# Retention queries projected with channels on partitions, rotary tables from plain transposes, decays moved into the norm's constant and the values

## The chip, the cores and the metric

The kernel runs on one core of a Trainium2 chip. A core has five engines with instruction streams of their own: PE (TensorE, matrix products and transposes), DVE (VectorE), ACT (ScalarE), POOL (GpSimd) and SP (SyncE, which here only issues DMAs). On-chip memory has 128 partitions; PE writes into PSUM, of which the kernel uses eight banks of 128 x 512 floats. The metric is the device time of one execution in microseconds, lower is better; a kernel's time is the median of its runs.

## The reference

Two layers of a decoder trunk on one sequence of 1024 tokens with 1024 channels. In each layer a normed and modulated h (1024 x 1024) goes through one projection whose columns feed three head groups: A, sliding-window attention with rotary; B, retention; C, gated linear attention. The gated outputs are joined, projected by `w_out`, normed, scaled by a gate and added to x. The part that the change touches is retention, with 4 heads of 64 channels and chunks of 128 tokens:

```python
rq = apply_rotary(rq.reshape(B, S, RET_HEADS, RET_DK), positions, ret_freq)
rk = apply_rotary(rk.reshape(B, S, RET_HEADS, RET_DK), positions, ret_freq)
r = retention(rq, rk, rv.reshape(B, S, RET_HEADS, RET_DV))
r_out = rms_norm(r).reshape(B, S, RET_W) * jax.nn.silu(rg)
# retention, per chunk and head, gamma = 1 - 2**(-5 - head), k scaled by 64**-0.5:
dmask = jnp.where(diff >= 0, jnp.exp(log_g[:, None, None] * jnp.maximum(diff, 0.0)), 0.0)
sc = jnp.einsum('bhid,bhjd->bhij', qi, ki) * dmask
intra = jnp.einsum('bhij,bhjv->bhiv', sc, vi)
inter = jnp.einsum('bhid,bhdv->bhiv', qi * q_decay, state)
new_state = chunk_decay * state + jnp.einsum('bhjd,bhjv->bhdv', ki * k_decay, vi)
```

`apply_rotary` turns each head's two halves of 32 channels by the token's angle: (x1 cos - x2 sin, x2 cos + x1 sin). The decay between token j and token i of a chunk is gamma**(i - j), so it can be split into a factor of i and a factor of j.

## The kernel before, in words

**Tiles.** The 1024 tokens are 8 tiles of 128 (`t`), or 4 pairs (`p`), or 2 halves (`hf`). h is kept transposed, channels on partitions, as a high and a low float32r part (`hT[(l, p)]`, 256 tokens per pair); the weights are split the same way, in blocks of 256 columns. Every projection is three passes (high x high, low x high, high x low; `PASSES`, L608) over 8 blocks of 128 channels, 24 products for one result.

Two forms of projection exist. `project` (L619) keeps h in the array and streams the weights: the result has 128 tokens on partitions and 256 channels along the row. `project_T` (L626) keeps 128 columns of the weights and streams 512 tokens: the result has channels on partitions.

**The order of a layer** (`layer`, L1466): output gates of C and B (`do_gates`), the retention pairs, C's projections and cores, keys and values of A, A's queries (`attn_rot`, L859), A's gates, then the output projection. In the last layer that product is done by a Strassen-like scheme in `last_output`.

**Who sets the order.** PE's instructions run in the order in which the program writes them down. This order comes from a small planner in the program: `clk` adds up a cost of each PE instruction (`mult`, L164; `transp`, L179), and generators (`job`) give back by `yield` how long after their last step their next PE step is due; the delays stand in the table `L` (L1677). `pump()` (L210) is called every 7 products inside a projection and runs the jobs that are due. `flag` and `await_flag` tie steps to one another: a `yield (0.0, name)` waits for a flag. On the other engines the compiler orders instructions by its own estimate, within the order of priority in which the program writes them. SP's queue takes its issues in order, each when its buffers are ready.

**Buffers.** `t2` (128 x 512, 10 of them), `t1` (128 x 256, 8), `st` (staging for weights, 5), `mm` (3 PSUM banks for projections), `aux` (5 banks for the rest), `mix_tile` (two large tiles), and `kT0`, `kT1` (one each of 128 x 1024, in turn for x, gaT, A's keys and the sums of the last layer).

**Tables.** `tables` (L411) works out sine and cosine of all angles into `sincos` (token on partition; for each tile sine then cosine, 32 rotary columns of A, then 32 of B), with 16 DVE operations of 512 columns on four `t2` tiles and two on ACT. `tables_T` (L444) makes A's tables with channels on partitions: for each pair a DVE copy repeats the 32 columns for 4 heads (L449), four transposes (L455), a copy on ACT with the factor 0.125 (L457), and a store into `tabS` in DRAM (L458). `attn_rot` loads them back in halves, two DMAs of 256 KB a time (L864). A's queries then are turned as whole banks: bank times cosine (L870), bank times sine (L871), a difference (L873), a sum (L874), a copy on ACT (L877); four DMAs of 32 partitions swap the halves into place (`qst`, L880).

**Retention** (L1502 to L1520). For each pair, the blocks rq, rk and rv are projected in this order, two tiles each, token on partition. `ret_rot` (L1154) turns a tile of q or k by `rotary` (L817: five DVE operations, L823 to L828) and multiplies it by its decay (L1157): gamma**(i+1) for q (`qdec`), 0.125 gamma**-(i+1) for k (`kdec`). A tile of v is copied by ACT. After each tile of v the job `ret_core` (L1160) starts:

```python
        for j in range(2):
            transp(pt[:, j * P:(j + 1) * P], q[:, j * P:(j + 1) * P], ident)
            transp(pt[:, (2 + j) * P:(3 + j) * P], k[:, j * P:(j + 1) * P], ident)
        tt_ = t2()
        ...
        copy("rT", tt_, pt)
```

ACT copies the four transposes into `tt_`, the scores k'q are made with 64 rows each (L1175), DVE masks them (L1179), PE adds scores x v and q x state (L1187, L1189), makes the state's increment (L1194), and DVE adds it and decays the state. `head_norm_gate` (L970) squares, reduces, makes the reciprocal root (`rstd_of`, L632, with a constant epsilon) and multiplies by the gate.

After the last tile of each block the next weights are asked for: `load` (L508) puts four pieces on a queue; each piece is a DMA of 256 KB into an `st` tile, a conversion to the high part (L149, ACT or DVE) and a subtraction to the low part (L533, DVE or POOL).

## Time and profile before

| | |
|---|---|
| median of 3 runs (lowest, highest) | 996.02 us (995.09, 997.33) |
| the profiled execution, its own time | 996.31 us |
| its span, first to last instruction | 994.6 us |
| granted TensorE clock, mean | 0.991 |
| transposes of `t` tiles on PE | 292 |
| DMAs issued: loads from `tabS`, swaps of q's halves | 16, 32 |
| SP queue, share of 16 DMA engines | 44.5% |

The prediction quotes rows of the profile. In a row of a group stand line, engine, operation, output<-input, shapes and count, then busy microseconds and the mean nanoseconds of one, then the engine's idle time before them with what ended it. A row of the timeline or of the chain starts with start and length in microseconds from the start of the span; x4 means four instructions merged. A row of the waits gives total microseconds, number of times and the longest. A row of stretches gives the stretch, its length, the busy time and instruction count of PE, PEld (the loading of the stationary operand), DVE, ACT and POOL, then the clock, the DMA share and GB/s. Matmuls overlap, and their ends are modelled: their pace is read from starts, not from durations.

### The profile page before, as it was taken

To read this page: it belongs to the slowest core of one execution; us is meant where nothing else is said; L and a number is where in the kernel's file an instruction comes from. 1 tells how busy PE (TensorE), PEld (TensorE's weight loads), DVE (VectorE), ACT (ScalarE), POOL (GpSimd) and SP (SyncE) were. 2 spreads that over 40 slices of the span, in tenths; PEclk is the share of its full clock that TensorE was granted. 3 is DMA by queue.
4 is the path that set the end of the run, shared out by engine and by line. 5 is a ranking of instruction groups with operands and counts; after the bars stand their busy time and mean duration, and the time that the engine had idled before them with its cause. 6 is when DMAs were issued, how large, how long until landed. Compare 5 with 4: busy or idle time off the path is not lost.

```text
span 994.6 us, 19641 instructions
## 1 busy us (share of the span) xinstructions
PE 965.7 (97%) x7133; PEld 824.3 (83%) x7133; DVE 683.2 (69%) x1679; ACT 409.3 (41%) x1152; POOL 246.3 (25%) x310
## 2 busy tenths in 40 slices
PE   5899999999999999999999999999999999999996
PEld 1599999888998777778889999988999877777785
DVE  3779857677766777664677286775766577567876
ACT  2477312233332656632555332133333257574222
POOL 2322001233310234420124101113322034545000
PEclk8899999999999999999999999999999999999999
DMA  9843513523135355587555241352122434378883
GB/s 321 290 138 97 159 44 115 177 86 121 61 100 166 91 157 168 170 274 239 189 170 171 69 150 38 118 157 83 53 93 86 127 91 133 112 235 266 267 262 139
DMA packets 112305, 148.77 MB, mean 150 GB/s; under 512 B 12065, under 2 KB 63821, under 8 KB 112209
## 3 DMA queue, kind: packets, MB, share of 16 engines
q1 hardware_dynamic: 106512, 137.96, 44.5%
q10 hardware_dynamic: 5696, 9.56, 2.6%
q8 instruction: 56, 0.92, 0.4%
q14 instruction: 41, 0.33, 0.1%
HBM read 109.20 MB, written 36.18 MB: 146 GB/s over the span
## 4 chain that ended last, share of the span: by engine, by line
PE 80%; DVE 7%; DMA 7%; issue 2%; POOL 1%; ACT 1%; SPq 0%; ACTq 0%; POOLq 0%; DVEq 0%
PE mm L165 61%; PE aux L165 14%; PE aux L180 5%; DMA st<-in_w_in_dram 2%; POOL sm L635 1%; DMA t<-aoS 1%; DMA st<-in_w_last_dram 1%; DMA xk<-in_x_dram 1%; DVE arena L533 1%; DMA a<-mixS 1%; DVE t L1248 0%; DVE t L328 0%; DMA t<-in_x_dram 0%; DMA t<-xs 0%; DMA mixS<-t 0%
## 5 line engine op out<-in xcount | busy, mean ns | idle before, releaser
L165 PE MATMUL mm<-arena 128*128 128x256 f32 (+2 forms) x1824 | 299.9, 318 | 1.8 <-ACT arena L704 1.8
L165 PE MATMUL mm<-arena,arena 128*128 128x256 f32 (+2 forms) x1824 | 298.2, 316 | 0.0
L165 PEld LDWEIGHTS mm<-arena 128*128 128x128 f32 x1824 | 255.5, 191 | 26.0 <-issue 3.3
L165 PEld LDWEIGHTS mm<-arena,arena 128*128 128x128 f32 x1824 | 252.2, 188 | 24.3 <-issue 3.7
L635 POOL TENSOR_TENSOR sm<-sm,mhalf 128x1 f32<-128x1 f32 (+1 forms) x64 | 55.8, 872 | 335.9 <-DVE sm L634 317.8
L165 PE MATMUL mm<-arena,mx 128*128 128x512 f32 (+1 forms) x564 | 130.6, 387 | 0.5 <-ACT kept L1341 0.5
L165 PEld LDWEIGHTS mm<-arena,mx 128*128 128x128 f32 x564 | 101.4, 188 | 24.7 <-issue 1.9
L149 ACT ACTIVATE t<-aux 128x256 f32<-128x256 f32 (+2 forms) x124 | 55.8, 468 | 73.8 <-PE aux L180 62.2
L149 ACT ACTIVATE arena<-st 128x512 fp32r<-128x512 f32 x94 | 56.2, 627 | 53.2 <-DMA st<-in_w_in_dram 19.4
L929 POOL TENSOR_TENSOR smx<-smx,sm 128x512 f32<-128x512 f32 x32 | 36.1, 1129 | 125.7 <-DVE sm L928 118.0
L533 POOL TENSOR_TENSOR arena<-st,arena 128x512 fp32r<-128x512 f32 x31 | 42.7, 1378 | 79.7 <-ACT arena L149 72.9
L533 DVE TENSOR_TENSOR arena<-st,arena 128x512 fp32r<-128x512 f32 x77 | 58.0, 775 | 5.2 <-ACT arena L149 3.3
L925 ACT ACTIVATE smx<-smx,sm 128x129 f32<-128x129 f32 x128 | 49.9, 393 | 25.9 <-DVE sm L922 25.7
L364 DVE SCALAR_TENSOR_TENSOR acc<-st,c_act,acc 128x512 f32<-128x512 f32 x60 | 46.7, 778 | 16.9 <-DMA st<-in_w_mod_dram 16.5
L180 PE MATMUL aux<-c_ident,t 128*128 128x128 f32 (+1 forms) x292 | 48.2, 282 | 5.4 <-DVE t L666 5.0
L180 PEld LDWEIGHTS aux<-c_ident,t 128*128 128x128 f32 (+1 forms) x292 | 35.0, 144 | 12.4 <-DVE t L666 6.9
L698 ACT ACTIVATE t<-aux,mod,mod 128x128 f32<-128x128 f32 x68 | 25.9, 459 | 43.0 <-DVE t L1248 18.1
L165 PEld LDWEIGHTS aux<-t,mx 32*128 32x128 f32 (+1 forms) x896 | 39.5, 187 | 3.9 <-issue 2.1
L973 ACT ACTIVATE t<-aux 128x256 f32<-128x256 f32 x32 | 12.3, 383 | 73.6 <-PE aux L165 65.0
L165 PE MATMUL aux<-t,mx 32*128 32x32 f32 (+1 forms) x896 | 40.7, 272 | 0.0
L920 DVE COPY_PREDICATED smx<-c_curmask,aux 128x256 f32<-128x256 int32 x64 | 25.4, 446 | 19.5 <-ACT smx L149 17.2
L1248 DVE SCALAR_TENSOR_TENSOR t<-t,sm,t 128x512 f32<-128x512 f32 x32 | 24.0, 780 | 18.2 <-DMA t<-in_x_dram 10.8
(224 smaller groups left out, 1387.7 us busy)
## 6 DMA issues: line engine op xcount, KB each, us to landing
st<-in_w_in_dram SPq DMA_DIRECT2D x96, 256.0 KB, 3.8
st<-in_w_mod_dram SPq DMA_DIRECT2D x64, 256.0 KB, 3.1
mx<-mixS SPq DMA_DIRECT2D x20, 512.0 KB, 4.9
mixS<-t SPq DMA_DIRECT2D x72, 128.0 KB, 3.7
st<-in_w_last_dram SPq DMA_DIRECT2D x36, 256.0 KB, 3.8
wm<-in_w_mod_dram SPq DMA_DIRECT2D x12, 512.0 KB, 7.0
t<-in_x_dram SPq DMA_DIRECT2D x24, 256.0 KB, 4.9
t<-tabS SPq DMA_DIRECT2D x16, 256.0 KB, 4.6
```

The source lines that it names most:

```text
L149: A.activation(dst, src, AF.Copy)
L165: T.matmul(dst, lhsT, rhs, start=start, stop=stop)
L180: T.transpose(dst, src, idn)
L364: V.scalar_tensor_tensor(acc, wt, c_act[:, k:k + 1], acc, ALU.mult, ALU.add)
L533: e.tensor_tensor(lo, st, f(hi), ALU.subtract)
L635: G.tensor_tensor(r, r, mhalf[:, :w], ALU.pow)
L698: A.activation(hf[:, ks], at[kt], AF.Identity, scale=gain, bias=shift)
L920: V.copy_predicated(sv, curmask.unsqueeze(1).to_broadcast((P, 2, P)), pv[:, :, n // P - 1, :])
L925: A.activation(sm[:, h, :], sm[:, h, :], AF.Exp, bias=mx[:, h:h + 1], accum_out=sums[:, h:h + 1])
L929: eng("pn").tensor_tensor(sm[:, :, 0:128], sm[:, :, 0:128], rs.unsqueeze(2).to_broadcast((P, 4, P)), ALU.mult)
L973: A.activation(sq, po, AF.Square)
L1248: V.scalar_tensor_tensor(xt[j], yg[j], r, xt[j], ALU.mult, ALU.add)
```

## The change

Six parts:

1. **q of retention** is projected by a new form, `project_P`: 128 columns of the weights in the array, 256 tokens of the pair streaming, two results in the two halves of one bank. The columns of rq are permuted on the host, so that the first result holds the first halves of all heads and the second the second halves. `ret_q` turns the bank with tables in four DVE operations, ACT copies it to a tile `rqT` (in the buffers kT0 for pairs 0 and 1, kT1 for pairs 2 and 3), and four DMAs (`qst`) swap the halves so that each head's 64 channels lie together. A flag falls due 6.5 planner units later (`rq1`).
2. **`ret_core`** transposes k alone, ACT copies 256 columns, and the scores and the product with the state read q from `rqT`, behind a wait for that flag.
3. **Decays.** q and k are no longer multiplied by a decay. v is, on DVE, by gamma**-(i+1) (`vdec`), in place of ACT's copy. The factor of i goes into the norm's epsilon, 4 EPS gamma**(-2(i+1)) (`reps`), since the head norm divides a common factor out; 0.125 comes with the tables.
4. **Tables** are transposed as `sincos` holds them: 8 transposes of 128 x 128 in two groups, two ACT copies, two stores into `tabS`, now 128 rows (sine for A, sine for B, cosine for A, cosine for B, 32 each) by 1024 tokens. The DVE copies (L449) are gone. A load repeats 32 rows for four groups of 32 partitions, with four DMAs (`tab_load`): eight of 64 KB in `attn_rot`, eight of 32 KB in `ret_q`.
5. **The work tiles of `tables`** come out of one `mix_tile` instead of four `t2`, and its first operation is put behind the last modulation on DVE (`mark[3]`).
6. **Delays** in `L`: `tb1` 24.5 to 20.0, `tt1` 8.0 to 3.0, `tt2` 1.75 to 2.0, `rq1` 6.5 new.

The core of the diff:

```diff
-    c["qdec"] = (gam[None, :] ** (i[:, None] + 1.0)).astype(f)
-    c["kdec"] = (0.125 * gam[None, :] ** (-(i[:, None] + 1.0))).astype(f)
+    c["reps"] = (4.0 * EPS * gam[None, :] ** (-2.0 * (i[:, None] + 1.0))).astype(f)
+    c["vdec"] = (gam[None, :] ** (-(i[:, None] + 1.0))).astype(f)
...
-        ang = t2()
-        V.tensor_tensor(ang.rearrange("p (t k) -> p t k", t=NT), posf.unsqueeze(2).to_broadcast((P, NT, 64)),
-                        freq.unsqueeze(1).to_broadcast((P, NT, 64)), ALU.mult)
+        tmp = mix_tile(F32).rearrange("p a k q -> p (a k q)").rearrange("p (i n) -> p i n", i=4)
+        ang, nn, n2, red = (tmp[:, i] for i in range(4))
+        with tc.issue_after(mark[3].ins):
+            V.tensor_tensor(ang.rearrange("p (t k) -> p t k", t=NT), posf.unsqueeze(2).to_broadcast((P, NT, 64)),
+                            freq.unsqueeze(1).to_broadcast((P, NT, 64)), ALU.mult)
...
+        for i in range(2):
+            yield L["tt1"] if i == 0 else L["tt2"]
             pt = aux()
-            for i in range(4):
-                transp(pt[:, i * P:(i + 1) * P], rep_[:, i * P:(i + 1) * P], ident)
+            for t in range(4):
+                transp(pt[:, t * P:(t + 1) * P], sincos[:, 4 * i + t].rearrange("p s k -> p (s k)"), ident)
             tb = t2()
             A.activation(tb, pt, AF.Copy, scale=0.125)
-            nc.sync.dma_start(tabS[p], tb.rearrange("p (s n) -> p s n", s=2))
+            nc.sync.dma_start(tabS[:, 512 * i:512 * i + 512], tb)
...
+    def project_P(pm, l, p, w, c):
+        h = hT[(l, p)]
+        accum(pm, lambda a, k: w[:, a, k, c:c + P], lambda b, k: h[:, b, k, 0:256])
...
+    def tab_load(d, r, c, n):
+        for h in range(4):
+            nc.sync.dma_start(d[32 * h:32 * h + 32], tabS[r:r + 32, c:c + n])
...
         for s, d in ((0, sn), (1, cs)):
-            nc.sync.dma_start(d.rearrange("p (s n) -> p s n", s=2),
-                              tabS[2 * hf:2 * hf + 2, :, s, :].rearrange("s p n -> p s n"))
+            tab_load(d, 64 * s, 512 * hf, 512)
...
+    def ret_q(l, p, w):
+        tab = t2()
+        for i in range(2):
+            tab_load(tab[:, 256 * i:256 * i + 256], 64 * i + 32, 256 * p, 256)
+        pm = mm()
+        for c in range(2):
+            project_P(pm[:, 256 * c:256 * c + 256], l, p, w, c * P)
...
+        u, x = t2(), t2()
+        V.tensor_tensor(two(u), two(pm), cs, ALU.mult)
+        V.tensor_tensor(two(x), two(pm), sn, ALU.mult)
+        V.tensor_tensor(u[:, 0:256], u[:, 0:256], x[:, 256:512], ALU.subtract)
+        V.tensor_tensor(u[:, 256:512], u[:, 256:512], x[:, 0:256], ALU.add)
+        if p % 2 == 0:
+            rqT[0] = gp.tile([P, NT * P], F32, tag=f"kT{p // 2}", name=nm("rq"), bufs=1)
+        q = rqT[0][:, 512 * (p % 2):512 * (p % 2) + 512]
+        A.activation(q, u, AF.Copy)
+        q, u = two(q), two(u)
+        for j in range(2):
+            for r in range(2):
+                dst, src = 64 * r + 32 * (1 - j), 64 * r + 32 * j
+                dma("qst", q[dst:dst + 32, j], u[src:src + 32, 1 - j])
+        flag(("rq", l, p), L["rq1"])
+        return q
...
         for j in range(2):
-            transp(pt[:, j * P:(j + 1) * P], q[:, j * P:(j + 1) * P], ident)
-            transp(pt[:, (2 + j) * P:(3 + j) * P], k[:, j * P:(j + 1) * P], ident)
-        tt_ = t2()
...
-        copy("rT", tt_, pt)
+            transp(pt[:, j * P:(j + 1) * P], k[:, j * P:(j + 1) * P], ident)
+        kTt = t1()
+        copy("rT", kTt, pt[:, 0:256])
+        yield (0.0, ("rq", l, t // 2))
...
-        yield from head_norm_gate(l, t, po[:, 0:256], sg, 4.0 / 64.0, 4.0 * EPS, 4)
+        yield from head_norm_gate(l, t, po[:, 0:256], sg, 4.0 / 64.0, reps, 4)
...
+            q = ret_q(l, p, used(l, "rq"))
+            pump()
+            if last:
+                load(l, "gqk")
+            ks = {}
+            for name in ("rk", "rv"):
...
                     if name == "rv":
                         v = t1()
-                        copy("rv", v, src)
-                        job(ret_core(l, t, rr[("rq", tt)], rr[("rk", tt)], v))
+                        V.tensor_tensor(h4(v), h4(src), vdec.unsqueeze(2).to_broadcast((P, 4, 64)), ALU.mult)
+                        job(ret_core(l, t, q, ks[tt], v))
                     else:
-                        rr[(name, tt)] = ret_rot(t, src, qdec if name == "rq" else kdec)
+                        ks[tt] = ret_k(t, src)
...
+    icols[RQ:RQ + 256] = RQ + np.arange(256).reshape(2, 2, 2, 32).transpose(2, 1, 0, 3).reshape(-1)
```

More of the change, by code (lines that the diff above doesn't have):

```diff
@@ L262, in trunk @@
     srS = dr.tile([NT, P, 256], F32, name="srS")
-    tabS = dr.tile([NP_, P, 2, 256], F32, name="tabS")
+    tabS = dr.tile([P, S], F32, name="tabS")
     modc = {}
@@ L429, in tables @@
         yield
-        red = t2()
         for i, cv in enumerate(cw_consts(1.0)):
@@ L767, in trunk @@
     hmask = cload("hmask")
-    qdec = cload("qdec")
-    kdec = cload("kdec")
+    reps = cload("reps")
+    vdec = cload("vdec")
     cdt = cload("cdt")
@@ L1151, in gla_out, with two, ret_k @@
         yield from head_norm_gate(l, t, po, gate, 1.0 / 64.0, EPS, 6)
-    def ret_rot(t, src, dec_):
+    def ret_q(l, p, w):
[5 more added lines that the diff above has]
+            project_P(pm[:, 256 * c:256 * c + 256], l, p, w, c * P)
+        def two(x):
+            return x.rearrange("p (c n) -> p c n", c=2)
+        sn, cs = (tab[:, 256 * i:256 * i + 256].unsqueeze(1).to_broadcast((P, 2, 256)) for i in range(2))
+        u, x = t2(), t2()
[14 more added lines that the diff above has]
+        return q
+    rqT = [None]
+    def ret_k(t, src):
         r = t1()
         rotary(r, src, 4, t, 1)
-        eng("rdec").tensor_tensor(h4(r), h4(r), dec_.unsqueeze(2).to_broadcast((P, 4, 64)), ALU.mult)
         return r
@@ L1503, in layer @@
             last = p == NP_ - 1
-            rr = {}
-            for name in ("rq", "rk", "rv"):
+            q = ret_q(l, p, used(l, "rq"))
[4 more added lines that the diff above has]
+            for name in ("rk", "rv"):
                 w = used(l, name)
@@ L1513, in layer @@
                         v = t1()
[L1514 to L1515 removed]
+                        V.tensor_tensor(h4(v), h4(src), vdec.unsqueeze(2).to_broadcast((P, 4, 64)), ALU.mult)
+                        job(ret_core(l, t, q, ks[tt], v))
                     else:
[L1517 removed]
+                        ks[tt] = ret_k(t, src)
                     pump()
                 if last:
[L1520 removed]
+                    load(l, {"rk": "gv", "rv": "kv"}[name])
         G.memset(stC, 0.0)
```

24 lines of the change are left out of this document (8 added, 16 removed).

## The prediction

> **What bounds the kernel now.** I read the page first: engines, then the chain that ended last.
>
> ```profile
> PE 965.7 (97%) x7133; PEld 824.3 (83%) x7133; DVE 683.2 (69%) x1679; ACT 409.3 (41%) x1152; POOL 246.3 (25%) x310
> ...
> PE 80%; DVE 7%; DMA 7%; issue 2%; POOL 1%; ACT 1%; SPq 0%; ACTq 0%; POOLq 0%; DVEq 0%
> ```
>
> PE is busy 97% of the span and makes 80% of the chain. So what PE is given to do counts almost in full, and what the other engines do counts only where PE waits for them. Next the weight-load row of PE in the timeline, around the ends of the two retention stages, which shows where PE waits there.
>
> ```profile
> 192.83 0.52 PEld L165 LDWEIGHTS aux<-t 64*128 64x128 f32 x8 [1.73 <-ACT t L149]
> ...
> 663.09 0.52 PEld L165 LDWEIGHTS aux<-t 64*128 64x128 f32 x8 [0.75 <-ACT t L149]
> ...
> 669.66 0.52 PEld L165 LDWEIGHTS aux<-t 64*128 64x128 f32 x8 [1.41 <-ACT t L149]
> ```
>
> These are the score products of `ret_core` (64 rows), which wait for ACT's copy of the transposes (the `rT` copy): 1.73 + 0.75 + 1.41 = 3.9 us in all. The chain of waits tells why ACT was late:
>
> ```profile
> 186.23 1.00 DVE arena L533 x2
> 187.24 4.07 DMA st<-in_w_in_dram
> ...
> 191.39 0.06 ACT arena L149
> ...
> 191.93 0.86 ACT t L149 x2
> ```
>
> DVE splits a weight block late, only then is the staging tile free, the next weight block takes 4.07 us to arrive, ACT stands at its conversion, and the `rT` copy is queued behind that. The fourth pair of each retention stage, taken as one stretch each, shows DVE nearly full:
>
> ```profile
> 166.30:187.20 20.90, 20.90 (x183) 20.51 (x183) 18.50 (x54) 6.02 (x13) 5.55 (x4) 1.00 0.42 133
> ...
> 641.00:662.00 21.00, 21.00 (x184) 20.76 (x182) 16.78 (x50) 5.98 (x13) 3.84 (x4) 1.00 0.38 119
> ```
>
> The third column after the length is DVE: 18.50 of 20.90 us and 16.78 of 21.00. PE has no pause in either stretch; its clock is full.
>
> **The change part by part.**
>
> *PE.* The transposes of q go: 2 of 4 in each `ret_core`, 16 of them (8 tiles, 2 layers), so 32. The tables need 8 transposes for 16. That is 40 fewer.
>
> ```profile
> L180 PE MATMUL aux<-c_ident,t 128*128 128x128 f32 (+1 forms) x292 | 48.2, 282 | 5.4 <-DVE t L666 5.0 <-DVE mx L1121 0.2
> ```
>
> ```profile
> 97.26 0.44 PE aux L180 x4
> ...
> 120.17 0.44 PE aux L180 x4
> ```
>
> The group gives 282 ns for one, but 292 x 282 would be 82 us and the group is busy 48.2: they overlap. The chain shows the pace: four of the tables take 0.44 us (97.26), and four in `ret_core` too (120.17), 0.11 us each. 40 x 0.11 = **-4.4 us**. The Trainium skill, page "TensorE: Matmul & The Clock Gate", section "Part 4: PE-mode transpose", gives about 275 ns for one in a kernel's context; as a duration the 282 ns agree with it, and by it as a cost the sum would be 40 x 0.275 = -11 us, an estimate from that page; the pace of 0.11 us disagrees. The last rival below is that case, worked out from the row.
>
> The projection of q changes sides (weights stationary, 256 tokens streaming), with the same 48 products of 256 columns for a pair.
>
> ```profile
> L165 PE MATMUL mm<-arena 128*128 128x256 f32 (+2 forms) x1824 | 299.9, 318 | 1.8 <-ACT arena L704 1.8
> L165 PE MATMUL mm<-arena,arena 128*128 128x256 f32 (+2 forms) x1824 | 298.2, 316 | 0.0
> ```
>
> These groups hold both kinds of projection, and 2 ns is all that parts them: 384 products x 2 ns bounds it at +-0.8 us. I take 0.
>
> *DVE.* Rows of the first retention stage, kept apart by shape, and from the whole run the product of a 512-wide bank with a table:
>
> ```profile
> L823 DVE TENSOR_TENSOR t<-mm,sincos 128x256 f32<-128x256 f32 x16 | 6.6, 414 | 1.9 <-PE mm L165 1.9
> ...
> L827 DVE TENSOR_TENSOR t<-t,tr 128x128 f32<-128x128 f32 x16 | 4.8, 300 | 0.0
> L828 DVE TENSOR_TENSOR t<-t,tr 128x128 f32<-128x128 f32 x16 | 4.5, 280 | 0.0
> L825 DVE TENSOR_TENSOR tr<-mm,sincos 128x128 f32<-128x128 f32 x16 | 4.5, 278 | 0.0
> L826 DVE TENSOR_TENSOR tr<-mm,sincos 128x128 f32<-128x128 f32 x16 | 4.4, 277 | 0.0
> ...
> L1157 DVE TENSOR_TENSOR t<-t,c_qdec 128x256 f32<-128x256 f32 x8 | 3.3, 418 | 0.1
> L1157 DVE TENSOR_TENSOR t<-t,c_kdec 128x256 f32<-128x256 f32 x8 | 3.3, 414 | 0.1
> L979 DVE TENSOR_TENSOR t<-t,t 128x256 f32<-128x256 f32 x6 | 2.9, 490 | 0.1
> L978 DVE TENSOR_TENSOR t<-aux,sm 128x256 f32<-128x256 f32 x6 | 2.5, 425 | 5.1 <-POOL sm L635 5.1
> ```
>
> ```profile
> L870 DVE TENSOR_TENSOR t<-mm,t 128x512 f32<-128x512 f32 x16 | 11.0, 688 | 15.5 <-PE mm L165 11.8 <-DMA t<-tabS 3.6
> ```
>
> For a pair, q cost 2 x (414 + 278 + 277 + 300 + 280 + 418) = 3.93 us and will cost 2 x 688 + 2 x 490 = 2.36. k loses 2 x 0.414 = 0.83. v gains a product from PSUM with a broadcast factor, as L978: 2 x 0.425 = 0.85, and ACT loses that copy. Sum per pair -1.6 us. Nothing of it is on PE's path by itself: it counts through the 3.9 us of waits above, which start from a DVE that is late in the fourth pair. By the point where v's products come, DVE is about 2 us ahead of today. The bounds are 0 (the waits stay, because the load's own 4.07 us or a new wait rules) and -3.9 (all go). I take the middle: **-2.0 us**. What is late next is the same `rT` copy behind the next weight block.
>
> *Table transposes.* The planner's delays change: tables start 4.5 us earlier (tb1), and from their end to the first transpose it waits 3.0 instead of 8.0 + 1.75 us.
>
> ```profile
> 69.27 0.68 DVE L414 TENSOR_TENSOR t<-sm,c_freq 128x512 f32<-128x512 f32 x1
> ...
> 92.27 0.43 DVE L442 TENSOR_SCALAR sincos<-sincos 128x512 f32<-128x512 f32 x1
> ```
>
> Today the tables take from 69.27 to 92.70, and PE transposes at 97.26 (above). A unit of the planner lasts longer than a microsecond: it counts 0.107 for a product of 256 columns, and
>
> ```profile
> 123.61 4.85 PE mm L165 x41
> ```
>
> gives 0.118, a factor of 1.1. So PE reaches the transposes 11.25 x 1.1 = 12.4 us earlier, at 84.9, and the tables start 5.0 earlier, at 64.3; if they again take 23.4 they end at 87.7 and PE, which works in a fixed order, waits 2.8 us. If they find a freer DVE (their tiles no longer wait for `t2` buffers) it waits for nothing. I take **+1.2 us**, between 0 and 2.8.
>
> *Table loads and q's swap, on SP's queue.* Attention's 16 loads become 64, retention adds 64 loads and 32 copies of q's halves; 4 stores become 2. That is 142 more issues on SP.
>
> ```profile
> 308.80 0.94 SPq L864 DMA_DIRECT2D t<-tabS  x2
> 310.88 2.50 SPq L154 DMA_DIRECT2D t<-t  x4
> ```
>
> ```profile
> 315.62 1.29 DVE L839 TENSOR_TENSOR mx<-t,mx 128x512 fp32r<-128x512 f32 x2
> ```
>
> ```profile
> 316.87 0.89 PE L165 MATMUL aux<-kT,mx 64*128 64x128 f32 x12
> ```
>
> One issue takes 0.47 (load) to 0.63 us (32 partitions to 32). In layer 0's attention the two loads at 308.80 stand ahead of q's copies at 310.88, and the first scores start at 316.87, just when DVE's split of q ends (315.62 + 1.29 = 316.91): no slack. Eight loads end at 308.80 + 8 x 0.47 = 312.6, so q's copies start 1.7 us later, and PE with them, if the order stays. If SP takes the loads earlier it is 0. I take **+1.0**; elsewhere in attention I price the loads at nothing, since they are issued ahead.
>
> In retention the new wait is PE's for q: after the 48 products come 2 x 0.688 + 2 x 0.49 on DVE, a copy on ACT, four issues, and the landing.
>
> ```profile
> L877 ACT ACTIVATE t<-t 128x512 f32<-128x512 f32 x16 | 9.9, 629 | 26.1 <-DVE t L874 23.7 <-DVE t L873 2.3
> ```
>
> ```profile
> t<-t SPq DMA_DIRECT2D x32, 64.0 KB, 2.0
> ```
>
> 2.36 + 0.63 + 2.50 + 2.0 = 7.5 us. PE has k's two tiles and v's first meanwhile, 72 x 0.118 = 8.5, and then the planner's 0.8 + 1.09 before the scores: 10.4 us. The spare is 2.9 us for DVE's and SP's arrears; I price it at **+0.6** (a miss in one pair of five by a microsecond or less). Queued behind q's copies on SP are weight loads; behind the scores on PE stands everything.
>
> The state in `rqT` takes buffers whose earlier readers are two pairs past (gaT), and the norm's constant becomes a tile in one small operation: nothing.
>
> **Sum.** -4.4 - 2.0 + 1.2 + 1.0 + 0.6 = -3.6 us. The profiled execution took 996.31 us (span 994.6 and 1.7 around it); the median of the runs is 996.02, 0.3 below it. So 992.7 for an execution like the profiled one, and **992.4** against the median.
>
> **Rivals.**
>
> 1. *The gain goes into the new waits* (all bounds at their dear end): -4.4 + 0 + 2.8 + 1.7 + 0.6 = +0.7, 996.7. For it: PE works in a fixed order, and the first scores of layer 0 show a place without slack. Against it: DVE does get lighter just where the waits start.
>
> 2. *Slower: PE waits for q in the pairs of retention.* The place is the first score product of each pair, behind q's copies on SP. What speaks for it is how SP stands today:
>
> ```profile
> SPq L154 <- ACT t L149: 127.0, 44, 12.4
> SPq L154 <- DVE arena L533: 78.6, 36, 10.6
> ```
>
> SP takes its issues in order, and waits 127.0 / 44 = 2.9 us on average for an ACT copy and 2.2 for a weight split, at the longest 10.6 to 12.4. One average wait ahead of q's copies eats the spare of 2.9; a late DVE as well, and PE stalls. It decides from 0.53 us of stall a pair: 8 pairs, 4.2 us, which is the sum without the 0.6. With 1.0 to 1.5 us in each pair the kernel takes 996.0 - 4.2 + 8 to 12, some 1000 to 1004. Against it: a wait of SP holds q's copies only where its order puts them behind it, and the copies of attention, which have the same place in the code, reach their scores with none or little to spare but in time (316.87 above). Four issues take 2.50 us against 2.0 for a landing. The Trainium skill, page "DMA: Bandwidth & Descriptors", section "Issuing engines are not separate DMA queues", calls the issuing time usually small against the transfer; the trace disagrees, and by that page this rival would have half its chance.
>
> 3. *All waits go*: -4.4 - 3.9, and nothing comes back: 987.7.
>
> 4. *A transpose costs PE its whole duration*: 40 x 0.282 = -11.3 with the other terms as forecast, 985.5. The pace of 0.11 us in two places of the chain speaks against it. The Trainium skill's 275 ns of the same page would be such a cost.
>
> **How the numbers follow.** This kernel's measurement tells about 0.2%, 2 us. Forecast, 988.5 to 994.0: 0.52. Rivals 3 and 4, below 988.5: 0.11 and 0.02. Rival 1, 994.0 to 998.0: 0.17. Rival 2, above 998.0: 0.18. So faster 0.65, same 0.17, slower 0.18. The unknown terms at their cheap ends, with 0.8 for the projections, give -4.4 - 3.9 - 0.8 = 986.9, and at their dear ends 996.7 + 0.8; the range goes down to 986.5 (0.04 left below) and on into rival 2 to 999.0 (0.14 above). The forecast's own range is 988.5 to 994.0.
>
> **What would show it.** Right: 40 fewer transposes on PE (the group of 292 at about 252) at 0.11 us in the chain; L1157 gone; PE's waits for ACT's `rT` copy at the end of both retention stages shorter than 3.9 us together. Wrong: waits of PE for `t<-t` or a copy behind it in retention (rival 2), for ACT or DVE at table transposes before 100 us by more than 2.8, or at the first attention scores by more than 1.7; or a pace of the q products other than 0.118 us.

## The result, and the profile after

The changed kernel takes **1010.38 us** (median of 4 runs, 1005.85 to 1013.22) against 996.67 for the kernel before on the same chip (995.09 to 997.73): a ratio of 1.0135, 95% interval 1.0094 to 1.0175. It is slower by 13.7 us where 3.6 us of gain were forecast, and outside of the range. The profiled execution took 1005.85 us, its span 1004.1, against 996.31 and 994.6; the reading below is made on 9.5 us of the loss, and the other runs lose more.

The page of the changed kernel, with the lines that answer to those of before:

```profile
span 1004.1 us, 19689 instructions
...
PE 966.9 (96%) x7093; PEld 823.5 (82%) x7093; DVE 675.2 (67%) x1611; ACT 403.3 (40%) x1143; POOL 246.1 (25%) x310
...
PEclk8999999999999999999999999999999999999998
...
PE 62%; DVE 7%; DMA 5%; issue 2%; POOL 1%; SPq 1%; ACT 1%; POOLq 0%; DVEq 0%
```

Every engine except PE has less to do, as the change says, and PE has 40 instructions less and yet 1.2 us more of busy time: something makes its instructions longer. Its idle time (span less busy time) grew from 28.9 to 37.2 us; these 8.3 us and the 1.2 are the 9.5 us. The groups of PE show the transposes gone:

```profile
L180 PE MATMUL aux<-c_ident,t 128*128 128x128 f32 (+1 forms) x244 | 41.7, 283 | 8.3 <-DVE t L667 7.4 <-DVE mx L1125 0.7
```

292 became 252 (244 here, and 8 of the table in a group of their own, busy for 1.2 us); 48.2 us of busy time became 42.9. So the removed work is really gone. Next PE's waits between 100 and 960 us, behind the start-up (us in total, times, longest):

```profile
PE aux L165 <- DVE t L1212: 3.5, 2, 2.7
PE aux L165 <- ACT t L149: 3.3, 1, 3.3
PE aux L180 <- DVE t L667: 1.6, 1, 1.6
...
PE aux L165 <- DVE sm L279: 0.9, 1, 0.9
PE aux L180 <- DVE mx L1125: 0.7, 1, 0.7
```

The same view of the kernel before:

```profile
PE aux L165 <- ACT t L149: 3.0, 3, 1.3
...
PE aux L165 <- DVE t L1179: 0.4, 1, 0.4
```

The first two lines belong to the retention stages: `rT` (ACT L149) and the masking of the scores (DVE L1212, before L1179). They were 3.4 us, all at the ends of the two stages, and are 6.8: 6.0 at the ends and 0.9 at 168 us. The other three are new and lie in places that the diff doesn't touch: the stage of gated linear attention (L279 at 240 us, L1125 at 263 us) and the output projection (L667 at 508 us). The timelines of PE, ACT and DVE at the two ends (start, length, engine; in brackets the idle time before and what ended it):

```profile
189.63 1.80 PE L165 MATMUL mm<-arena,arena 128*128 128x512 f32 x7
194.76 0.72 PE L165 MATMUL aux<-rq,t 64*128 64x128 f32 x8 [3.33 <-ACT t L149]
...
675.15 1.11 PE L165 MATMUL aux<-t,t 128*128 128x64 f32 x4 [2.65 <-DVE t L1212]
```

```profile
191.85 0.63 ACT L149 ACTIVATE arena<-st 128x512 fp32r<-128x512 f32 x1 [0.34 <-DMA st<-in_w_in_dram]
192.39 0.36 ACT L149 ACTIVATE t<-aux 128x256 fp32r<-128x256 f32 x1
193.81 0.63 ACT L149 ACTIVATE arena<-st 128x512 fp32r<-128x512 f32 x1 [1.06 <-DMA st<-in_w_in_dram]
194.35 0.36 ACT L149 ACTIVATE t<-aux 128x256 f32<-128x256 f32 x1
```

```profile
670.82 0.75 DVE L364 SCALAR_TENSOR_TENSOR acc<-st,c_act,acc 128x512 f32<-128x512 f32 x1 [1.62 <-DMA st<-in_w_mod_dram]
672.85 1.12 DVE L151 CAST arena<-st 128x512 fp32r<-128x512 f32 x1 [1.27 <-DMA st<-in_w_in_dram]
674.07 0.69 DVE L527 TENSOR_TENSOR arena<-st,arena 128x512 fp32r<-128x512 f32 x1
674.68 0.75 DVE L1212 TENSOR_TENSOR t<-aux,c_causal 128x256 f32<-128x256 f32 x2
```

On both engines a small operation that PE waits for (`rT`, the mask) stands in an in-order queue behind a conversion of a weight whose transfer has not landed. It is the mechanism that the prediction described, only that it got worse. The last view is the one that I had not looked at closely enough: windows around two of these waits (length, busy us of PE, PEld, DVE, ACT and POOL, granted clock of PE, DMA share, GB/s). The granted clock is the share of its full speed at which PE may run; half clock is a value of about 0.5.

```profile
237.60:241.00 3.40, 2.53 (x56) 1.87 (x54) 3.22 (x10) 1.83 (x4) 0.00 (x0) 1.00 0.27 91
241.00:244.40 3.40, 3.40 (x26) 2.95 (x23) 1.89 (x7) 1.80 (x7) 0.00 (x0) 0.51 0.75 248
...
671.10:674.50 3.40, 1.40 (x9) 1.03 (x7) 2.02 (x3) 1.01 (x2) 1.26 (x1) 1.00 0.99 341
674.50:681.40 6.90, 6.25 (x26) 5.48 (x27) 5.24 (x14) 2.16 (x4) 2.27 (x2) 0.51 0.77 242
```

After a window in which PE was busy for 1.40 of 3.40 us the clock is at half for about 6.8 us: the wait of 2.65 us costs up to 6.8 / 2 = 3.4 us more. The stretch at 241 us costs up to 1.7. The two, 5.1 us, are most of what makes PE's busy time 1.2 us longer where the transposes alone would make it 4.4 shorter. The four runs of the changed kernel have mean clocks of 0.987, 0.984, 0.980 and 0.980 and take 1005.85, 1010.71, 1013.22 and 1010.04 us; the profiled execution before has 0.991. By the mean clock, half clock takes (1 - 0.980) x 1009 = 20 us in the last two and 0.009 x 995 = 9 before. Not all of this is lost, since some of it falls where PE waits anyway: before, the clock is full from 46 to 985 us, and all of its half clock lies in the start and at the end.

### The profile page after: what moved, and what is told of

The parts are those of the page before. It is cut to its first block, busy times and chain, and to the rows that moved or that the text cites. A ratio compares the mean times of both kernels' runs of the same rounds, so it can differ in the third digit from the quotient of the medians.

```text
span 1004.1 us, 19689 instructions
## 1 busy us (share of the span) xinstructions
PE 966.9 (96%) x7093; PEld 823.5 (82%) x7093; DVE 675.2 (67%) x1611; ACT 403.3 (40%) x1143; POOL 246.1 (25%) x310
## 4 chain that ended last, share of the span: by engine, by line
PE 62%; DVE 7%; DMA 5%; issue 2%; POOL 1%; SPq 1%; ACT 1%; POOLq 0%; DVEq 0%
PE mm L165 46%; PE aux L165 12%; PE aux L180 3%; DMA t<-mixF 1%; DMA st<-in_w_last_dram 1%; DMA st<-in_w_mod_dram 1%; SPq L154 1%; POOL sm L636 1%; DVE arena L527 1%; DMA t<-xs 1%; DVE t L1281 1%; DMA t<-aoS 0%; DMA st<-in_w_in_dram 0%; DVE arena L709 0%; DVE mx L1100 0%
## 5 line engine op out<-in xcount | busy, mean ns | idle before, releaser
L165 PE MATMUL mm<-arena 128*128 128x256 f32 (+2 forms) x1824 | 299.6, 318 | 2.1 <-ACT arena L705 1.8
L165 PE MATMUL mm<-arena,arena 128*128 128x256 f32 (+2 forms) x1824 | 298.3, 316 | 0.0
L149 ACT ACTIVATE t<-aux 128x256 f32<-128x256 f32 (+2 forms) x124 | 52.0, 438 | 92.5 <-PE aux L180 74.4
L149 ACT ACTIVATE arena<-st 128x512 fp32r<-128x512 f32 x94 | 56.2, 627 | 61.5 <-DMA st<-in_w_in_dram 26.0
L527 DVE TENSOR_TENSOR arena<-st,arena 128x512 fp32r<-128x512 f32 x77 | 61.6, 820 | 6.7 <-ACT arena L149 3.9
L364 DVE SCALAR_TENSOR_TENSOR acc<-st,c_act,acc 128x512 f32<-128x512 f32 x60 | 45.3, 755 | 22.9 <-DMA st<-in_w_mod_dram 20.5
L180 PE MATMUL aux<-c_ident,t 128*128 128x128 f32 (+1 forms) x244 | 41.7, 283 | 8.3 <-DVE t L667 7.4
L180 PEld LDWEIGHTS aux<-c_ident,t 128*128 128x128 f32 (+1 forms) x244 | 29.3, 144 | 15.9 <-DVE t L667 7.5
```

The costliest lines, as they stand in the source:

```text
L149: A.activation(dst, src, AF.Copy)
L165: T.matmul(dst, lhsT, rhs, start=start, stop=stop)
L180: T.transpose(dst, src, idn)
L364: V.scalar_tensor_tensor(acc, wt, c_act[:, k:k + 1], acc, ALU.mult, ALU.add)
L527: e.tensor_tensor(lo, st, f(hi), ALU.subtract)
```

## The experiments

All ratios are to the kernel before, run on the same chip beside each; the last column is PE's wait for `rT` and masks in the retention stages (same view as above), of the one profiled execution. Differences in microseconds are between medians. The runs stand on several chips, on which the kernel before has medians of 995.91 to 997.79 us, and a difference between chips is uncertain by as much. The code of the edits is shortened.

| run | what it is | median us | ratio, 95% interval | waits us |
|---|---|---|---|---|
| after | the change | 1010.38 | 1.0135 (1.0094-1.0175) | 6.8 |
| e1 | decays alone | 996.08 | 0.9992 (0.9976-1.0009) | 1.5 |
| e2 | tables alone | 997.60 | 1.0000 (0.9984-1.0015) | 2.6 |
| e3 | decays and tables | 996.60 | 0.9992 (0.9975-1.0008) | 1.5 |
| e4 | after, query pieces on ACT's queue | 1010.17 | 1.0141 (1.0097-1.0185) | 6.4 |
| e5 | after, 32 idle transposes | 1003.93 | 1.0068 (1.0044-1.0092) | 7.7 |
| e6 | e3 without query transposes | 1003.04 | 1.0075 (1.0043-1.0107) | 3.3 |
| e7 | after, 40 small transfers fewer per stage | 1006.49 | 1.0105 (1.0075-1.0135) | 5.0 |
| e8 | e3, 32 table loads more per stage | 994.60 | 0.9979 (0.9965-0.9993) | 1.1 |
| e9 | after, planner's clock padded | 1001.83 | 1.0039 (1.0021-1.0057) | 7.2 |
| e10 | e3, planner's clock not counting them | 1002.03 | 1.0043 (1.0025-1.0062) | 2.7 |
| e11 | after, `rT` on DVE | 1011.85 | 1.0140 (1.0106-1.0174) | 6.6 |
| e12 | e9, last scores planned 4 us later | 996.19 | 0.9995 (0.9979-1.0010) | 1.7 |
| e13 | e9, one weight's loads asked for later | 1003.18 | 1.0063 (1.0040-1.0085) | 7.7 |
| e14 | e12 and e13 | 995.98 | 0.9993 (0.9980-1.0006) | 1.6 |
| e15 | e12, two more due times | 991.18 | 0.9949 (0.9930-0.9968) | 0 |
| e16 | before, with the ends of e15 | 994.39 | 0.9984 (0.9970-0.9999) | 0 |
| e17 | e3, with the due times of e15 | 992.98 | 0.9965 (0.9950-0.9979) | 0 |
| e18 | e15 without the padding | 994.51 | 0.9976 (0.9960-0.9991) | 0.2 |

**Which part costs: e1 to e4.** Theory S at this point was rival 2 of the prediction widened: table and query pieces in SP's queue hold up weight loads.

```
e1, e3  - r = rotary(q or k) * decay      + r = rotary(q or k); v = pm * vdec; eps = reps
e2, e3  + tables(), tables_T(), tab_load() of the change; attention loads by tab_load
e4      - "qst": "S"                      + "qst": "A"
```

> The kernel before with the decays alone moved: queries and keys lose their multiplication by the decay on DVE (32 of 0.42 us in the two retention stages), values are multiplied on DVE instead of being copied on ACT, and the constant in the norm takes the query's part. Queries still go through transposes, tables and queues are those of before. Theory S (the loss of the change is in SP's queue: table pieces and query pieces ahead of weight loads): this part has no DMA, so it keeps or beats the time before, 993 to 997 us. Theory T (the loss is in the tables, built early and loaded in pieces): the same, 993 to 997. Theory R (any edit moves the written-out order of PE and the scheduler's order of the other engines, and the loss is scattered stalls that come from that): a time away from the one before by 3 us or more, up or down, with new stalls outside of the retention stages.

> The kernel before with the tables alone changed: 8 plain transposes of the table started some 12 us earlier, and attention loads its two tables in eight pieces. Retention is that of before. Theory S: only the stall at the table's transposes (1.8 us in the changed kernel) less the saved 8 transposes (0.9 us), so 996 to 999 us. Theory T: most of the loss of 14 us, 1004 to 1010. Theory R: as in the first run, 3 us or more away from before with stalls in other places.

> The decays and the tables together on the kernel before; only the query's projection with channels on partitions, its rotation and its copies between partitions are left out, so queries are rotated as before and transposed on PE. What stands between this and the changed kernel is the query part alone. Theory S: 994 to 999 us, and the 11 to 16 us up to the changed kernel's 1010 belong to the query part. Theory T: 1004 to 1010, the query part being worth nothing or a gain of 3.5 us (32 transposes of 0.11 us). Theory R: not the sum of the first two runs.

> The changed kernel with the 16 copies of query pieces between partitions in each retention stage issued from ACT's queue instead of SP's: the same transfers, but 16 issues of 0.59 us and the wait for ACT's copy ahead of them (5.5 us in the first retention stage) are gone from SP's queue, where weight loads stand behind them. Theory S: weight loads go out earlier, the stalls at both ends of the retention stages (3.3 us and 2.65 us of PE's wait) shrink to 1 to 2 us, and the time is 1002 to 1008 against 1010. Theory T: no difference, 1009 to 1011, or slower if ACT's own queue suffers from the issues. Theory that the transfers themselves (1 KB rows, 32 partitions each) slow the weight loads: no difference, since the same bytes go over the same engines.

The first three keep the time before within 0.2%, so theory T falls and the whole loss comes with the query part: 0.9992 to 1.0135. Theory R fell as stated, since no part of the three moved by 3 us; it came back narrower (e9). e4 takes 16 issues of 0.59 us and their wait out of SP's queue and gains nothing, which speaks against S, though ACT now has to issue them, and a gain on SP could be lost there; e7 takes the transfers out altogether.

**Work, plan or transfers: e5 to e8.** Theory L: PE, with 3.5 us less to do, runs ahead of the weight loads.

```
e5  + transp(pt[:, (2 + j) * P:(3 + j) * P], k[...], ident)       (never read)
e6  - transp(pt[...], q[...], ident); qT = tt_[:, 0:256]          + qT = kTt
e7  + if p == 0: load the table once into a tile of its own       - dma("qst", ...)
e8  + tab = t2(); tab_load(tab..., 256) x2 at each pair           (never read)
```

> The changed kernel with 32 idle transposes put back at the place where the queries' transposes were (each retention tile transposes its two key halves once more into a half of the PSUM tile that nobody reads): PE has as much to do as before, everything else is the changed kernel. Theory L (PE gets ahead of the weight loads in the retention stage by the 3.5 us of the missing transposes, waits at its end, and the gated linear attention stage behind it runs short of work and loses the clock): the waits go and the time falls, 996 to 1003 us, although PE has 3.5 us more to do. Theory S (table and query pieces in SP's queue delay the weight loads): the same waits, 1010 to 1014. Theory C (the query's own chain, DVE and ACT copy and buffers, is late): 1010 to 1014.

> The third run's kernel (decays and tables moved, queries rotated with rows on partitions) with the queries' transposes left out and the transposed keys taken in their place, so the scores are keys with keys: 32 transposes and half of the copies rT less, and none of the query part's DMAs, DVE forms or buffers. Theory L: PE gets ahead as in the changed kernel and the same loss shows, 1003 to 1012 us. Theories S and C: nothing of the query part is there, so it keeps the saved transposes, 992 to 996.

> The changed kernel with 40 of the 48 small transfers of each retention stage taken out of SP's queue: the rotation table is loaded for the first pair and used for all four (so the other pairs are rotated by wrong angles), and the copies of query pieces between partitions are left out (so half of each query is not rearranged); the eight table loads of the first pair stay, and the table no longer takes one of the ten tiles t. Theory S: most of the loss goes, 994 to 1000 us. Theory L: PE is as early as in the changed kernel, 1004 to 1012. Theory C: 1004 to 1010.

> The third run's kernel (996.6 us, no query part) with the 32 table pieces of each retention stage loaded into a tile t that nobody reads: the same number of issues of 0.42 us in SP's queue and the same buffer taken, and nothing else of the query part. Theory S: a part of the loss shows, 1000 to 1006 us. Theories L and C: 996 to 999.

Giving PE 3.5 us of useless work makes the changed kernel *faster* by 6 us (e5, 1 us above L's range), and taking the same transposes from e3, without any of the query part, makes it *slower* by 6. Transfers do neither: 32 loads more per stage are no loss (e8, below all three ranges), 40 fewer leave 1.0105 of 1.0135, their intervals overlapping (e7). So S falls as the main cause, and C cannot explain e6. But L is only half borne out: in e5 the waits at the ends did not shrink (7.7 us); what went were the waits at 240 and 263 us, and the one at 508 us fell from 1.6 to 0.5.

**The plan by itself: e9 to e11.**

```
e9   + clk[0] += 0.109    (at each of the two key transposes)
e10  + clk[0] -= 0.109    (at each of the two query transposes)
e11  - "rT": "A"          + "rT": "V"
```

> The changed kernel with no instruction added or taken away; only the planner's clock, by which PE's order is written out, is moved on by 0.22 us at each retention tile, as if the queries' transposes were still there. It tells two halves of theory L apart. Theory LP (the plan: with 3.5 us less counted, the due times tuned for the old kernel fall at other products, and the stalls at 240, 263 and 508 us come from that order): these three stalls go as they did with the idle transposes, and the time is 1003 to 1007 us. Theory LW (the work: PE really is too early for the weight loads, whatever the plan says): the same as the changed kernel, 1008 to 1012.

> The third run's kernel (996.6 us: decays and tables moved, queries transposed on PE as before) with the same instructions, but the planner's clock doesn't count the queries' transposes. PE has its old work and the order that is planned without it. Theory LP: the stalls in the gated linear attention stage (about 240 and 263 us) appear, 999 to 1005 us. Theory LW: 995 to 998.

> The changed kernel with the copy rT of the transposed keys on DVE instead of ACT. At the end of both retention stages PE waits for this copy, which stands in ACT's queue behind a conversion of a weight that has not landed. Theory L: DVE's queue holds conversions of the same weights, so the wait moves to DVE and stays for the most part, 1007 to 1013 us. The theory that the loss is ACT's queue order alone: the stall of 3.3 us at 191 us and what the clock loses behind it go, 1002 to 1006.

e9 and the changed kernel issue the same instructions, and e9 is 8.6 us faster; e10 and e3 issue the same, and e10 is 5.4 us slower. LW falls and LP holds, though e9 came out 1.2 us below LP's range. PE's timeline at 263 us shows how. In e3:

```profile
258.71 0.44 PE L180 MATMUL aux<-c_ident,t 128*128 128x128 f32 x2
258.91 1.07 PE L165 MATMUL mm<-arena,arena 128*128 128x256 f32 x7
260.19 0.33 PE L180 MATMUL aux<-c_ident,t 128*128 128x128 f32 x1 [0.20 <-DVE mx L1121]
```

In e10:

```profile
260.26 0.44 PE L180 MATMUL aux<-c_ident,t 128*128 128x128 f32 x2
261.42 0.33 PE L180 MATMUL aux<-c_ident,t 128*128 128x128 f32 x1 [0.73 <-DVE mx L1121]
```

`accum` lets other work in only after every 7 products (`CHUNK`). With 0.22 us less counted for each tile a due time falls one group of 7 earlier: the group that covered the wait for DVE is not there, and PE waits 0.73 instead of 0.20 us. At 508 us the results have 512 columns, and there `accum` lets other work in after every 4 products. Between the last transposes and those that wait stand 44 products in e3 and e9, 36 in e10 and the changed kernel: two groups less, 8 x 0.235 = 1.9 us, and the waits are 1.53 and 1.59 us. At 240 us the order moves the other way. In the changed kernel and in e9:

```profile
232.03 6.04 PE L165 MATMUL mm<-arena 128*128 128x256 f32 x30
238.01 0.23 PE L180 MATMUL aux<-c_ident,t 16*128 16x16 f32 x1
239.82 1.47 PE L165 MATMUL aux<-t,mx 32*128 32x32 f32 x41 [0.87 <-DVE sm L279]
```

```profile
231.21 1.08 PE L165 MATMUL mm<-arena 128*128 128x256 f32 x7
232.23 0.23 PE L180 MATMUL aux<-c_ident,t 16*128 16x16 f32 x1
232.39 4.27 PE L165 MATMUL mm<-arena 128*128 128x256 f32 x19
```

A small transpose for the modulation, in e9 written out behind 7 products, now stands behind 30, just ahead of the scores of gated linear attention, and these wait until DVE has copied its result (L279).

These three waits come to 3.2 us, and the two profiled executions are 4.0 us apart (spans of 1004.1 and 1000.1), not 8.6. The rest lies in executions without a profile and goes with their clock: 0.980 to 0.984 in the other three of the changed kernel, 0.983 to 0.988 in the eleven of e9. Where such a clock can come from is seen in e4, which has the changed kernel's order on PE: its profiled execution (1016.74 us, clock 0.973) stood at half clock for 31 us between 196 and 282 us. For the changed kernel itself this is argued, not shown.

e11 shows that the ends are not a matter of ACT's queue alone. With `rT` on DVE the waits are 6.6 us, and 2.4 more at 194 us for which the profile names no releaser. On DVE, too, operations on weights that have not landed stand ahead of the mask or of `rT`: at 680 us a conversion (L151) after 1.83 us of waiting for `in_w_in`, at 168 us L364 after 2.76 us for `in_w_mod`.

**The ends of the retention stages: e12 to e14.** Two theories for the 5 us that e9 still is above e3: A, `rT` stands behind the conversion of a weight that has not landed, and behind the idle time the clock falls to half; B, the query's own chain is late there. e9's windows at its two ends show what is left:

```profile
187.90:191.30 3.40, 1.20 (x6) 0.61 (x4) 2.34 (x6) 1.47 (x3) 0.00 (x0) 1.00 1.01 288
191.30:198.10 6.80, 5.65 (x21) 4.66 (x22) 1.61 (x4) 0.97 (x3) 1.27 (x1) 0.50 0.69 223
662.40:665.80 3.40, 0.88 (x8) 0.67 (x6) 0.73 (x2) 0.00 (x0) 0.00 (x0) 0.99 0.86 174
665.80:672.60 6.80, 5.49 (x21) 4.49 (x22) 3.79 (x8) 2.53 (x6) 1.72 (x1) 0.50 0.78 272
```

```
e12  - yield lat("rc2", l)     + yield lat("rc2", l) + (4.0 if t >= 6 else 0.0)
e13  load(l, "kv") moved from the last value product to behind do_gqk(0, 0)
```

> The kernel of the ninth run (planner's clock padded, 1001.8 us) with the scores of the last two retention tiles of each layer planned 4 us later, so that PE has products of the next stage to do while the copy rT waits behind a weight's conversion. Theory A: the waits of 3.8 us at 189 and 663 us shrink to under 1.5 us and the stretches at half clock behind them go (3.4 us each), so 992 to 998 us. Theory B: the query is no later than before, but its scores are, nothing is gained: 1000 to 1004.

> The kernel of the ninth run with the load of the attention's key and value weights (four of 256 KB, used only some 30 us later) asked for after the first product group of the next stage instead of at the last value product of the retention stage. Theory A: the conversions that stand ahead of the last rT are fewer, the waits at the ends of the retention stages shrink by half or more and the clock stays up, 994 to 999 us. Theory B: 1000 to 1004. If the key and value weights come late for their own use, a new wait shows near 250 us.

> Both of the last two edits on the kernel of the ninth run. Theory A: as the better of the two or better by up to 2 us, 991 to 997 us, which would beat the kernel before (996.5) by the saved transposes. Theory B: 1000 to 1004.

e12 gains 5.6 us without touching a transfer, by giving PE other products while `rT` waits; the same stretch of time is then full:

```profile
186.00:196.00 10.00, 10.00 (x56) 7.56 (x55) 6.59 (x14) 2.99 (x7) 1.40 (x2) 1.00 0.74 226
```

At the second end 1.7 us of waits and half clock behind them are left. With the padding and this one due time the changed kernel is where the kernel before is, and e14, with e13's edit on top, is no different. e13 missed: four loads less in the stretch changed nothing (7.7 us of waits), so the half of theory A that blames the number of loads is not borne out.

**A version that beats both: e15 to e18.**

```
e15  + yield max(lat("rc3", l), 5.87) if t >= 6 else lat("rc3", l);  "tt1": 3.0 -> 5.5    (on e12)
```

> The kernel of the twelfth run (the changed kernel, planner's clock padded, last scores 4 us later) with two more due times moved: the product that follows the last scores of the second layer is planned 5.87 us behind them as in the first layer (1.9 before), and the table's transposes 2.5 us later. Theory A (what is left are waits that the plan can move): the waits at 86 us (1.8) and 668 us (1.9) go with the half clock behind the latter, 990 to 995 us, below the kernel before. Theory B: no better than the twelfth run, 995 to 998.

> The kernel before with the same two edits at its own retention ends: the scores of the last two retention tiles 4 us later and what follows them at least 5.87 us behind. If the ends of the retention stages are bound by the weight loads whatever the query does: its waits of 1.7 us at 191 and 1.5 and 0.8 us near 668 go, 991 to 995 us. If the wait there is a matter of the changed kernel alone: 995 to 998.

> The third run's kernel (decays and tables moved, queries transposed as before) with the due times of the fifteenth run (last scores 4 us later, what follows them 5.87, the table's transposes 2.5 us later), and no padding, since the transposes are there. If the query part pays for itself under a fitting plan, this is above the fifteenth run by about the 32 transposes, 993.5 to 996 us; if the fifteenth run's gain came from the due times alone, 990 to 992.

> The fifteenth run's kernel without the padded clock: the changed kernel with the three due times moved. Theory L (plan and ends are two causes): the stalls at 240, 263 and 508 us of the changed kernel are there, 995 to 1002 us. If the ends alone were the cause: 990 to 993.

e15 takes 991.18 us, 0.51% below the kernel before (0.32 to 0.70). PE's busy time in e15 and, in the second fence, in e16:

```profile
PE 960.9 (97%) x7093; PEld 818.3 (83%) x7093; DVE 675.8 (68%) x1611; ACT 402.5 (41%) x1143; POOL 243.2 (25%) x310
```

```profile
PE 965.1 (97%) x7133; PEld 823.7 (83%) x7133; DVE 684.7 (69%) x1679; ACT 409.4 (41%) x1152; POOL 243.6 (25%) x310
```

The difference is 4.2 us, the 4.4 of the prediction's first term: with a plan that fits, the removed transposes do count. In time e15 is 3.2 us below e16, which ran beside it, and their intervals do not overlap; e15 has the table's due time moved besides. e16 itself is 0.16% below the kernel before (0.01 to 0.30) and has lost its waits at the ends, so these due times help without the change as well. How much of e15 is the query part stays open: e17, which lacks it, is 0.16% above, with overlapping intervals. Without the padding (e18) 2.7 us of the gain are lost, and PE waits 1.6 us for L667 again; the intervals overlap here too. 994.51 us lies between the two ranges that were expected, so with the ends re-planned the padding is worth less than the 8.6 us of e9, and how much less is not settled.

## Why the prediction was wrong

- **The transposes, -4.4: right as work.** 42.9 for 48.2 us in the groups, 4.2 us of PE between e15 and e16. Rival 4 (0.282 us each) falls with it.
- **The projection's other side, 0: right.** Its two groups take 299.6 and 298.3 us, before 299.9 and 298.2. The 48 products of the first pair's q start 0.119 us apart (41 of them from 105.06 to 109.95 us).
- **DVE, -1.6 us for a pair: right in size.** The group's rows of the first retention stage, one instruction a pair each, and the values':

```profile
L1551 DVE TENSOR_TENSOR t<-mm,c_vdec 128x256 f32<-128x256 f32 x7 | 2.9, 417 | 2.5 <-PE mm L165 2.5
L1171 DVE TENSOR_TENSOR t<-mm,t 128x512 f32<-128x512 f32 x4 | 2.8, 689 | 2.7 <-PE mm L165 2.7
L1172 DVE TENSOR_TENSOR t<-mm,t 128x512 f32<-128x512 f32 x4 | 2.7, 681 | 0.0
...
L1173 DVE TENSOR_TENSOR t<-t,t 128x256 f32<-128x256 f32 x4 | 1.7, 418 | 0.0
L1174 DVE TENSOR_TENSOR t<-t,t 128x256 f32<-128x256 f32 x4 | 1.7, 416 | 0.0
```

  0.689 + 0.681 + 0.418 + 0.416 = 2.20 us for q, 2.36 forecast. In the two retention stages (103 to 187 and 578 to 662 us) DVE's busy time fell by 5.9 and 5.8 us, 1.5 a pair.
- **The step that failed first: "it counts through the 3.9 us of waits above ... I take the middle: -2.0 us".** The waits doubled (3.4 to 6.8 us by PE's own rows; the 3.9 were read from the weight loads' row) although DVE was lighter. Their chain starts at weights that have not landed, and what decides is where the plan puts the scores: a due time alone takes e9's 7.2 us of waits to 1.7 (e12). I had taken the chain's first link (a late DVE) for its cause.
- **The step that was missing: the plan.** The sum has no term for it. I knew that PE works in an order written out by a planner, and used that for the table's transposes alone; that the planner counts the removed transposes too, so that steps tuned for the old order come out behind other groups of products, I did not ask. It is worth 8.6 us on the changed kernel and 5.4 on e3, and some 2.7 once the ends are re-planned (e15 and e18, intervals overlapping).
- **The clock.** I wrote "its clock is full" of two stretches and priced no wait above its own length. A wait of 2.65 us brought about 6.8 us of half clock.
- **Table transposes, +1.2 (0 to 2.8): within bounds, 1.76 us, by luck.** The tables started at 55.3 us, not 64.3, and ended at 88.0, so they took 32.7 us, not 23.4; the two errors cancel. PE was there at 86.4 us (84.9 forecast). The profile names an ACT copy (L1024), which ended 0.05 us behind the table's last operation:

```profile
88.17 0.63 PE L180 MATMUL aux<-c_ident,sincos 128*128 128x128 f32 x4 [1.76 <-ACT t L1024]
```

- **Attention's loads, +1.0: nothing.** The first scores of layer 0 have no wait in front of them, and e2 keeps the time before.

```profile
322.58 0.89 PE L165 MATMUL aux<-kT,mx 64*128 64x128 f32 x12
```

- **The wait for q, +0.6, and rival 2.** Rival 2's time (1000 to 1004) came nearest, but not for its reason: PE has no wait for `rq<-t`, and e4, which takes q's copies out of SP's queue, changes nothing. Its price of a stall in every pair was not paid; the loss sits at two ends and in stages that the diff doesn't touch. None of the signs that I had named for being wrong appeared in the profiled execution: the loss came by a path that was not on the list.

**What stays open**: why the ends are worse with the query part at all. Without e12's edit, the kernels that lack the query part have 1.1 to 3.4 us of waits in the retention stages, those that have it 5.0 to 7.7. The query's copies on SP (e4), the missing work (e5), ACT's queue (e11) and the loads of one weight (e13) each fail to explain it; e7, without 40 of the transfers, has 5.0. A combination was not tried.

## What to carry to other kernels

Where an engine's order is written out by a planner, removing an instruction also moves the plan: run the change once with the old time still counted before judging it, and re-tune the due times behind it. The waits at the ends went when other work was planned into them; a lighter DVE and a move of the late copy to the other engine had not removed them. And read the granted clock in windows around each wait: a wait of under 3 us can cost as much again in what runs behind it.

## What the runs showed of the hardware

- **The clock goes by the activity in a window, not by one gap, and busy time is not the whole of it.** Half clock came mostly in stretches of about 3.4 or 6.8 us. It followed windows with 1.40 (after), 1.20 and 0.88 us (e9) of PE busy in 3.40, but not this pair of the changed kernel, where a wait of 3.33 us is spread over two windows:

```profile
189.80:193.20 3.40, 1.64 (x7) 0.96 (x6) 3.05 (x8) 1.53 (x3) 0.00 (x0) 1.00 0.84 266
193.20:196.70 3.50, 1.94 (x14) 1.59 (x15) 1.10 (x4) 0.90 (x2) 1.27 (x1) 1.00 0.89 272
```

  At 241 us half clock followed a window with 2.53 us of busy time, most of whose instructions were products of 32 x 32. In e7 it followed a window (222.1 to 225.5 us) in which PE was busy for 3.33 of 3.40 us, again mostly with such products. Small products seem to count for less, which no run tested. The Trainium skill, page "TensorE: Matmul & The Clock Gate", section "Part 1: The HAM clock gate", describes a free-running window of 3.4 us whose activity sets the clock; the trace agrees with that. Section "Why this matters for your kernels" of that page allows gaps up to about 3 us; the wait of 2.65 us up to 675 disagrees.
- **A POOL instruction can hold DVE.** Moving the table's temporaries into `mx` put POOL's clearing of that tile beside the last table operation: DVE's L441 took 1.90 us, the same operation before (L442) 0.43. In e2, e3, e9, e12, e15 and e17 it took 1.91 us, each time beside such a clearing.

```profile
85.94 1.80 POOL L792 MEMSET mx<- 128x2048 f32 x1 [5.64 <-ACT sincos L438]
```

```profile
86.12 1.90 DVE L441 TENSOR_SCALAR sincos<-sincos 128x512 f32<-128x512 f32 x1
```

  They end within 0.3 us of each other. The Trainium skill, page "SBUF — State Buffer", section "Who interferes with whom", says that the two engines share a port pair, that whoever issues first holds it for the whole instruction, and that `tensor_scalar` can need it, in a mode that uses two ports. The trace agrees with the lock (1.90 against 1.80 us); whether L441 ran in that mode no run here shows.
